# The down projection of a decoder layer: other sums around its seven products, the weight sums made by DMAs in DRAM

## The chip, the cores and the metric

The kernel runs on one core of one Trainium2 chip. The metric is the device time of one execution in microseconds (us), median over several. The core has five engines that run their own instruction queues in order: TensorE (PE, with its weight loads PEld), VectorE (DVE), ScalarE (ACT), GpSimd (POOL) and SyncE (SP). SP, ACT and POOL also issue DMAs.

## The reference, cut to what matters

One decoder layer: a token mixer, a cross-attention and a gated MLP. The change touches the last matrix product, `(silu(a) * b) @ w_down`, that is 1024 x 2816 times 2816 x 1024.

```python
def conv_glu_ffn(h, w_up, conv_w, conv_b, w_down):
    u = causal_dwconv(h @ w_up, conv_w) + conv_b
    a, b = jnp.split(u, 2, axis=-1)
    return (jax.nn.silu(a) * b) @ w_down
...
    y = conv_glu_ffn(rmsnorm(h, g[4]), ffn_w_up[l], ffn_conv_w[l], ffn_conv_b[l], ffn_w_down[l])
    h = h + rmsnorm(y, g[5])
```

The input projection, `z = h @ w_in` at the layer's start, is where the change puts new DMAs.

## The kernel before

All data is float32. A product of two float32 matrices is made of three matmuls (`mm3`, lines 238 to 241): each operand is split into a high part in float32r, which ACT copies out, and a low part, which DVE makes by a subtraction, and the products high-high, high-low and low-high are added in PSUM. So each 128 x 512 operand tile costs ACT one copy and DVE one subtraction before TensorE can use it.

The stages that matter here run in this order.

**Input projection** (loop at line 670, 22 steps in `in_order`). Each step multiplies one 128-column slice of `w_in` with the whole normed input. `weight` (line 154) loads the weights two steps ahead and splits them into a tile of tag `w`, of which there are four (line 145), so a tile is used again four steps later. DVE also computes the depthwise convolution taps (line 355) and, behind step 13, a small triangular inverse, `base_inverse` (line 656), in a tile `b_ca` that POOL sets to zero and one first (lines 651, 652). From its end the scan of the next stage follows.

**Up projection** (lines 1243 to 1275). It writes the 22 tiles of the gated activations to DRAM (`mid_d`), which are 128 channels x 1024 tokens each.

**Down projection** (from line 1282). A is `mid_d`, B is `w_down`; both are cut in 2 x 2 blocks, for each of the 11 pairs of channel tiles `kp`. Seven block products (`PRODS`, a Strassen scheme) stand for the eight of the plain rule: 7 products x 11 steps x 4 row blocks x 3 = 924 matmuls of 512 columns. `down_operands` (line 1317) prepares one step: it loads one or two blocks of `w_down` by SP, adds them on DVE where there are two (line 1328), subtracts two blocks of A where there are two (line 1335), and splits the pair into a tile of tag `w` (lines 133 and 134 for a pair of sums, 1339 and 1340 otherwise). `a_block` loads each A block once, by SP. `fetch` keeps up to four steps prepared, and three steps of the last product in extra tiles (`EXTRA`). At the last step of a product `done` (line 1373) moves the four PSUM banks into the accumulators `yacc`, by ACT copies or DVE additions (line 1349). A list `pend` holds the normalisation work, which is put between the steps. The last six steps of the last product run one row block after the other, so that each block's end (line 1355) can begin while the next is multiplied.

The program is written in this order, and a planner places each engine's instructions, so neighbouring steps interleave. An engine that waits holds up all that is behind it in its queue.

Of the kernel before, what the change touches and what calls it, by code (L numbers as in the profile page):

```python
# [7 lines left out]
F32 = mybir.dt.float32  # L8
F32R = mybir.dt.float32r
I32 = mybir.dt.int32  # L10
AF = mybir.ActivationFunctionType
# [5 lines left out]
P = 128  # L17
T = 1024
D = 1024
# [50 lines left out]
def hybrid_layer(  # L70
# [69 lines left out]
    def raw_tile(shape, name):  # L140
        return wpool.tile(list(shape), F32, tag="raw", name=f"raw_{name}", bufs=2)
# [403 lines left out]
    def flush(keep=0):  # L545
        while len(pend) > keep:
            pend.pop(0)()
# [108 lines left out]
    def base_inverse():  # L656
# [9 lines left out]
            dve.tensor_tensor(bx[:, 0:k, k:B], bx[:, 0:k, k:B], t_, op=ALU.add)  # L666
        sync.dma_start(out=blocks(x_d), in_=bx)

    kinds = {"q": query, "k": key, "v": value, "g": gate, "a": glu_conv, "b": glu_gate}
# [597 lines left out]
    for j in range(PLAIN, NFF):  # L1267
# [6 lines left out]
        if j == PLAIN:  # L1274
# [4 lines left out]

    dr = ctx.enter_context(pool("dr", side="right"))
    dl = ctx.enter_context(pool("dl"))
    g5 = row_gain(5, gbp)
# [2 lines left out]
    ss5 = small(NC * 2, "ss5", bufs=1)  # L1287
    LAST = 6


    PRODS = (("M4", 0, ("22",), ("21", "11")), ("M3", 1, ("11",), ("12", "22")),
             ("M2", 0, ("22", "21"), ("11",)), ("M1", 1, ("11", "22"), ("11", "22")),
             ("M6", 0, ("21", "11"), ("11", "12")), ("M5", 0, ("11", "12"), ("22",)),
             ("M7", 1, ("12", "22"), ("21", "22")))
    ENDP = len(PRODS) - 1

    EXTRA = (5, 6, 7)
    res = {}

    def a_block(b, kp):  # L1300

        if (b, kp) not in res:
            if b == "21":
                if kp % 4 == 0:
                    g = dl.tile([P, 4, 512], F32, tag="a21", name=f"ma21_{kp}", bufs=3)
                    for i in range(4):
                        res[b, "t", kp + i] = g[:, i]
                t = res[b, "t", kp]
            else:
                t = (dr if b == "22" and kp < 8 else dl).tile([P, 512], F32, name=f"ma{b}_{kp}")  # L1310
            res[b, kp] = t
            sync.dma_start(out=t, in_=mid_d[2 * kp + int(b[1]) - 1][:, HS[int(b[0]) - 1]])
        return res[b, kp]

    n_step = [0]

    def down_operands(m, kp):
        name, _, ab, bb = PRODS[m]
        p, tag, bufs = (wpool, "raw", 2) if n_step[0] % 3 == 0 else (dr, "braw", 4)
        n_step[0] += 1  # L1320
        A_s = [a_block(b, kp) for b in ab]
        rb = p.tile([P, 2, 512], F32, tag=tag, name=f"rb{name}_{kp}", bufs=bufs)

        at = lambda b: w_down[2 * kp + int(b[0]) - 1][:, HS[int(b[1]) - 1]]
        sync.dma_start(out=rb[:, 1], in_=at(bb[0]))
        if len(bb) == 2:
            sync.dma_start(out=rb[:, 0], in_=at(bb[1]))
            dve.tensor_tensor(rb[:, 1], rb[:, 1], rb[:, 0], op=ALU.subtract if name == "M1" else ALU.add)
# [5 lines left out]
        if len(ab) == 2:  # L1334
            dve.tensor_tensor(rb[:, 0], A_s[0], A_s[1], op=ALU.subtract)
            split(w, rb)
        else:
            for i, r in enumerate((A_s[0], rb[:, 1])):
                act.activation(w[:, 0, i], r, AF.Copy)
                dve.tensor_tensor(w[:, 1, i], r, w[:, 0, i], op=ALU.subtract)  # L1340
        return w

    def square(t, n):
        jk = dl.tile([P, 512], F32, tag="junk", name="sqj", bufs=2)
        act.activation(jk, yacc[t][:, HS[n]], AF.Square, accum_out=ss5[:, 2 * t + n:2 * t + n + 1])

    def add_to(t, n, o, sign=1):
        y = yacc[t][:, HS[n]]
        dve.tensor_tensor(y, y, o, op=ALU.add if sign > 0 else ALU.subtract)

    def gained(t, n):
        y = yacc[t][:, HS[n]]
        dve.tensor_tensor(y, y, g5[:, HS[n]], op=ALU.mult)

    def final(t, fin, first):

# [9 lines left out]
        return s1  # L1366

    def residual(t, last=False):
        fin = raw_tile((P, D), f"fin{t}") if last else dl.tile([P, D], F32, tag="fin", name=f"fin{t}", bufs=2)
        sync.dma_start(out=fin, in_=h2_d[t])  # L1370
        return fin

    def done(name, q, o):

        lo, hi = q, q + 4
        if name == "M4":
            act.activation(yacc[hi][:, HS[0]], o, AF.Copy)
            act.activation(yacc[lo][:, HS[0]], o, AF.Copy)
        elif name == "M3":
            act.activation(yacc[lo][:, HS[1]], o, AF.Copy)  # L1380
            act.activation(yacc[hi][:, HS[1]], o, AF.Copy)
        elif name == "M2":
            add_to(hi, 0, o, -1)
            square(hi, 0)
            pend.append(lambda: gained(hi, 0))
        elif name == "M1":
            add_to(hi, 1, o)
        elif name == "M6":
            add_to(hi, 1, o)
            square(hi, 1)  # L1390
            pend.append(lambda: (gained(hi, 1), final(hi, residual(hi), 0)))
        elif name == "M5":
            add_to(lo, 0, o)
            add_to(lo, 1, o, -1)
            square(lo, 1)
            pend.append(lambda: gained(lo, 1))
        else:
            add_to(lo, 0, o)
            square(lo, 0)
            gained(lo, 0)  # L1400
            final(lo, fins.pop(lo), 1)

    fins = {}
    todo = [(m, kp) for m in range(ENDP) for kp in range(NP)]
# [13 lines left out]
        mm3(o, w[:, 0, 0, s], w[:, 1, 0, s], w[:, 0, 1], w[:, 1, 1], start, stop, onto)  # L1418

    banks = [None, None]  # L1420
    for m, (name, bset, _, _) in enumerate(PRODS):
        onto = name in ("M6", "M7")
        if not onto:
            banks[bset] = [psum("b", f"{name}_{q}") for q in range(4)]
        o = banks[bset]
# [9 lines left out]
                pend.pop(0)()  # L1435
    flush()
    fetch()
    fins.update({q: residual(q, q > 1) for q in range(4)})
    for q in range(4):
        for kp in range(NP - LAST, NP):  # L1440
            step_mm(banks[1][q], dops[ENDP, kp], q, False, kp == NP - 1, True)
        done("M7", q, banks[1][q])
    psum_es[0].close()


# [60 lines left out]
```

## Time and profile before

| | us |
|---|---|
| median of 3 runs | 1478.18 |
| the 3 runs | 1476.74, 1478.18, 1485.74 |
| the profiled execution, its own time | 1477.1 |
| its span, first to last instruction | 1475.1 |
| TensorE busy in the span | 1428.7 (97%) |
| VectorE busy | 1162.9 (79%) |
| ScalarE busy | 694.7 (47%) |
| GpSimd busy | 150.5 (10%) |

The span is the time from the first to the last instruction; 2.0 us of the execution lie around it. Matmuls are pipelined: one is shown as 0.39 us long, but the next begins some 0.227 us later. "Clock" is the granted TensorE clock, 1.00 is 2.4 GHz and 0.5 is 1.2 GHz.

### The profile page before, as it was taken

How to read it: one execution, taken by the hardware profiler on the slowest of the kernel's cores; microseconds unless marked ns; L12 is line 12 of the kernel's file. 1: busy time of each engine (PE TensorE's matmuls, PEld its weight loads, DVE VectorE, ACT ScalarE, POOL GpSimd, SP SyncE). 2: the span in 40 equal slices, each digit the busy share in tenths (PEclk: the TensorE clock that was granted, in tenths of full speed). 3: DMA queues.
4: the chain of work that ended last, by engine and by line, in shares of the span. 5: the costliest groups of instructions: out<-in, count | busy, mean ns of one | idle time of the engine just before them, and what ended most of it. 6: DMA issues, size and time to landing. Idle time of an engine off the chain costs nothing.

```text
span 1475.1 us, 19398 instructions
## 1 busy us (share of the span) xinstructions
PE 1428.7 (97%) x7087; PEld 1183.2 (80%) x7087; DVE 1162.9 (79%) x1971; ACT 694.7 (47%) x1309; POOL 150.5 (10%) x102
## 2 busy tenths in 40 slices
PE   6999999999999999999999999999999998999996
PEld 6878888888898878878788788888888886888875
DVE  6699999993567778743567988888888887879997
ACT  6526463642566545432534554444444444554442
POOL 0000000000000000000001233333333330000000
PEclk9999999999999999999999999999999999999998
DMA  7533233328756766410424522222222226985473
GB/s 251 165 96 94 79 101 80 120 99 266 245 169 204 244 223 189 127 68 1 157 101 143 171 100 72 86 86 79 79 72 86 86 84 202 343 291 187 144 251 112
DMA packets 121631, 212.01 MB, mean 144 GB/s; under 512 B 17440, under 2 KB 61120, under 8 KB 121536
## 3 DMA queue, kind: packets, MB, share of 16 engines
q1 hardware_dynamic: 97600, 159.13, 34.7%
q10 hardware_dynamic: 22976, 48.51, 8.8%
q0 software_dynamic: 960, 3.15, 0.7%
q8 instruction: 55, 0.90, 0.3%
q14 instruction: 40, 0.33, 0.1%
HBM read 156.73 MB, written 54.02 MB: 143 GB/s over the span
## 4 chain that ended last, share of the span: by engine, by line
PE 80%; DVE 7%; DMA 7%; ACT 2%; issue 2%; SPq 0%; DVEq 0%; ACTq 0%
PE st L239 9%; PE st L241 9%; PE st L240 8%; PE pj L241 6%; PE pj L239 6%; PE pj L240 6%; PE M L240 4%; PE M L241 3%; PE M L239 3%; PE y L240 2%; PE y L241 2%; PE y L239 2%; PE sc L240 1%; PE sc L241 1%; PE sc L239 1%
## 5 line engine op out<-in xcount | busy, mean ns | idle before, releaser
L241 PE MATMUL pj<-xT,w_in 128*128 128x512 f32 x384 | 150.3, 391 | 1.1 <-DVE w_in L134 1.1
L239 PE MATMUL pj<-xT,w_in 128*128 128x512 f32 x384 | 150.8, 393 | 0.1
L355 DVE SCALAR_TENSOR_TENSOR ca<-sg,par,ca 128x1023 f32<-128x1023 f32 (+18 forms) x120 | 149.9, 1264 | 1.1
L240 PE MATMUL pj<-xT,w_in 128*128 128x512 f32 x384 | 149.9, 390 | 0.0
L240 PE MATMUL M<-wM 128*128 128x512 f32 x308 | 121.3, 394 | 4.2 <-DVE wM L1340 2.7
L239 PE MATMUL st<-xT,wst 128*128 128x512 f32 x320 | 125.0, 391 | 0.0
L241 PE MATMUL st<-xT,wst 128*128 128x512 f32 x320 | 124.7, 390 | 0.0
L240 PE MATMUL st<-xT,wst 128*128 128x512 f32 x320 | 124.4, 389 | 0.0
L239 PE MATMUL M<-wM 128*128 128x512 f32 x308 | 119.5, 394 | 4.4 <-ACT wM L133 3.4
L241 PE MATMUL M<-wM 128*128 128x512 f32 x308 | 121.0, 393 | 0.0
L1156 DVE SCALAR_TENSOR_TENSOR ua<-ua,par 128x1023 f32<-128x1023 f32 x88 | 112.5, 1281 | 10.3 <-ACT ua L1154 7.4
L239 PE MATMUL st<-x,wst 128*128 128x512 f32 x240 | 96.8, 403 | 0.0
L241 PE MATMUL st<-x,wst 128*128 128x512 f32 x240 | 94.7, 394 | 0.0
L240 PE MATMUL st<-x,wst 128*128 128x512 f32 x240 | 94.2, 393 | 0.0
L133 ACT ACTIVATE wM<-rbM 128x1024 fp32r<-128x1024 f32 x55 | 57.9, 1062 | 74.8 <-PE M L241 51.8
L1186 DVE TENSOR_TENSOR wst<-sums,wst 128x512 fp32r<-128x512 f32 x80 | 63.5, 816 | 34.4 <-ACT wst L1185 34.3
L1185 ACT ACTIVATE wst<-sums 128x512 fp32r<-128x512 f32 x80 | 46.0, 620 | 91.1 <-POOL sums L1180 91.1
L241 PEld LDWEIGHTS pj<-xT,w_in 128*128 128x128 f32 x384 | 72.1, 188 | 15.9 <-DVE w_in L134 1.3
L239 PEld LDWEIGHTS pj<-xT,w_in 128*128 128x128 f32 x384 | 72.1, 188 | 14.9 <-ACT w_in L133 0.3
L240 PEld LDWEIGHTS pj<-xT,w_in 128*128 128x128 f32 x384 | 72.2, 188 | 14.5
L134 DVE TENSOR_TENSOR wM<-rbM,wM 128x1024 fp32r<-128x1024 f32 x55 | 66.7, 1221 | 8.7 <-ACT wM L133 8.7
L240 PEld LDWEIGHTS M<-wM 128*128 128x128 f32 x308 | 58.4, 190 | 18.2 <-DVE wM L1340 3.6
(383 smaller groups left out, 3566.0 us busy)
## 6 DMA issues: line engine op xcount, KB each, us to landing
rbM<-in_w_down SPq DMA_DIRECT2D x132, 256.0 KB, 3.9
raw_up<-in_w_up SPq DMA_DIRECT2D x44, 512.0 KB, 3.6
raw_in<-in_w_in SPq DMA_DIRECT2D x24, 512.0 KB, 3.7
mid_d<-ua ACTq DMA_DIRECT2D x22, 512.0 KB, 2.6
ma<-mid_d SPq DMA_DIRECT2D x44, 256.0 KB, 5.4
raw_kv<-in_w_kv SPq DMA_DIRECT2D x16, 512.0 KB, 4.0
h_d<-h ACTq DMA_DIRECT2D x16, 512.0 KB, 2.7
xr<-in_x ACTq DMA_DIRECT2D x8, 512.0 KB, 4.8
```

The lines of the kernel that those rows point to most:

```text
L133: act.activation(w[:, 0], raw, AF.Copy)
L134: dve.tensor_tensor(w[:, 1], raw, w[:, 0], op=ALU.subtract)
L239: pe.matmul(o, lhsT=wh, rhs=xh, start=start, stop=False, skip_group_check=onto)
L240: pe.matmul(o, lhsT=wh, rhs=xl, start=False, stop=False, skip_group_check=onto)
L241: pe.matmul(o, lhsT=wl, rhs=xh, start=False, stop=stop, skip_group_check=onto)
L355: dve.scalar_tensor_tensor(out=ca[:, d:], in0=sg[:, :T - d], scalar=par[:, wb + 30 - d:wb + 31 - d], in1=ca[:, d:], op0=ALU.mult, op1=ALU.add)
L1156: dve.scalar_tensor_tensor(out=a[:, d:], in0=u[:, :T - d], scalar=fw(2 - d), in1=a[:, d:], op0=ALU.mult, op1=ALU.add)
L1185: act.activation(w[:, i, 0], op[s], AF.Copy)
L1186: dve.tensor_tensor(w[:, i, 1], op[s], w[:, i, 0], op=ALU.subtract)
```

## The change

Another scheme with seven products: `P1` and `P2` add into the same PSUM banks, as do `P4` and `P5`, and `P6` and `P7`, each right after the other. On the A side the sums are made in place in the loaded blocks (two DVE operations in each step of `P2`, two in each of `P3`), and used again. On the B side four products take a sum of blocks (`T1` to `T4`). These 44 sums are made in DRAM, in 22 steps of the input projection: POOL reads a word of the step's weight tile (`mark`), and behind that issues four DMAs of 256 KB, plain copies and DMAs that add onto what is there (`accum_op`). The second to fourth of them read or add to what an earlier one has written. In the down projection SP loads one B tile in each step; POOL issues the loads of the A blocks "21" and "22". The row normalisation's multiply becomes a scalar_tensor_tensor with a sign.

```diff
+    td_d = [[dram.tile([P, 512], F32, name=f"td_d{k}_{i}") for i in range(4)] for k in range(NFF // 2)]
...
+    def weight_sums(n, name):
+        kp, part = divmod(n, 2)
+        if kp >= NFF // 2:
+            return
+        t1, t3, t2, t4 = td_d[kp]
+        dma = nc.gpsimd.dma_start
+        mark = small(1, "mark")
+        ins = nc.gpsimd.tensor_copy(mark, w_ready[name][:, 0, 0:1].bitcast(F32))
+        with tc.issue_after(ins.ins):
+            if part == 0:
+                dma(out=t1, in_=w_block(kp, "11"))
+                dma(out=t3, in_=w_block(kp, "12"))
+                dma(out=t1, in_=w_block(kp, "12"), accum_op=ALU.add)
+                dma(out=t3, in_=w_block(kp, "22"), accum_op=ALU.add)
+            else:
+                dma(out=t2, in_=t1)
+                dma(out=t2, in_=w_block(kp, "22"), accum_op=ALU.add)
+                dma(out=t4, in_=t2)
+                dma(out=t4, in_=w_block(kp, "21"), accum_op=ALU.add)
...
     for n, (kind, i) in enumerate(in_order):
         before = len(pend)
         kinds[kind](i)
+        weight_sums(n, f"in{col[kind] + i}")
...
+    PRODS = (("P1", 0, False, "11", "B11"), ("P2", 0, True, "12", "B21"), ("P3", 1, False, "S2", "T2"),
+             ("P4", 0, False, "21", "T1"), ("P5", 0, True, "12", "B22"), ("P6", 1, False, "11", "T3"),
+             ("P7", 1, True, "22", "T4"))
...
+    for kp in (0, 2):
+        g = raw_tile((P, 2, 512), f"ma11_{kp}")
...
+            (nc.gpsimd if b in ("21", "22") else sync).dma_start(
+                out=ma[b, kp], in_=mid_d[2 * kp + int(b[1]) - 1][:, HS[int(b[0]) - 1]])
...
+        rb = dr.tile([P, 512], F32, tag="braw", name=f"rb{name}_{kp}", bufs=6)
+        sync.dma_start(out=rb, in_=w_block(kp, b[1:]) if b[0] == "B" else
+                       td_d[kp][("T1", "T3", "T2", "T4").index(b)])
+        if name in ("P1", "P2"):
+            a_block({"P1": "21", "P2": "22"}[name], kp)
...
+        if name == "P3":
+            tt_(A, a_block("22", kp), a_block("11", kp), op=ALU.add)
+        for i, r in enumerate((A, rb)):
+            act.activation(w[:, 0, i], r, AF.Copy)
+            tt_(w[:, 1, i], r, w[:, 0, i], op=ALU.subtract)
+        if name == "P2":
+            tt_(a_block("11", kp), a_block("11", kp), a_block("21", kp), op=ALU.subtract)
+            tt_(a_block("21", kp), a_block("22", kp), a_block("21", kp), op=ALU.subtract)
+        elif name == "P3":
+            tt_(a_block("12", kp), A, a_block("12", kp), op=ALU.subtract)
...
+        if name == "P1":
             act.activation(yacc[hi][:, HS[0]], o, AF.Copy)
+        elif name == "P2":
             act.activation(yacc[lo][:, HS[0]], o, AF.Copy)
+            square(lo, 0)
+            pend.append(lambda: gained(lo, 0))
+        elif name == "P3":
+            add_to(hi, 0, o, alu=ALU.subtract)
+        elif name == "P4":
+            add_to(hi, 0, o, 1)
+        elif name == "P5":
+            dve.tensor_tensor(yacc[lo][:, HS[1]], yacc[hi][:, HS[0]], o, op=ALU.add)
...
-    for m, (name, bset, _, _) in enumerate(PRODS):
-        onto = name in ("M6", "M7")
+    for m, (name, bset, onto, _, _) in enumerate(PRODS):
```

## Rows read from the trace of the kernel before

**Rows 1.** Stretches of the down stage: busy us, PEclk, DMA share, GB/s
```profile
1250.00:1260.00 10.00, 7.46 (x32) 5.82 (x32) 10.00 (x16) 3.98 (x7) 0.00 (x0) 1.00 0.80 257
1260.00:1270.00 10.00, 10.00 (x46) 8.29 (x45) 8.59 (x14) 4.48 (x8) 0.00 (x0) 1.00 1.04 385
...
1420.00:1440.00 20.00, 16.25 (x69) 12.29 (x67) 19.99 (x34) 8.30 (x14) 0.00 (x0) 1.00 0.83 279
1440.00:1450.00 10.00, 8.83 (x28) 6.91 (x28) 10.00 (x14) 4.01 (x4) 0.00 (x0) 0.67 0.32 99
```

**Rows 2.** What TensorE waited for from 1236 us: total, times, longest
```profile
PE M L239 <- ACT wM L133: 3.4, 1, 3.4
PE M L240 <- DVE wM L1340: 2.7, 2, 1.7
PE M L240 <- DVE wM L134: 1.5, 1, 1.5
PE M L239 <- ACT wM L1339: 0.9, 1, 0.9
```

**Rows 3.** Timeline of TensorE, down stage: start, us, instruction, idle before and releaser
```profile
1242.71 0.50 PE L239 MATMUL M<-wM 128*128 128x512 f32 x1
...
1441.17 1.65 PE L239 MATMUL M<-wM 128*128 128x512 f32 x3 [3.43 <-ACT wM L133]
...
1463.82 0.39 PE L240 MATMUL M<-wM 128*128 128x512 f32 x1
...
1465.41 0.39 PE L241 MATMUL M<-wM 128*128 128x512 f32 x1
```

**Rows 4.** Groups by line, 1180 to 1475 us: busy, mean ns, idle before
```profile
L134 DVE TENSOR_TENSOR wM<-rbM,wM 128x1024 fp32r<-128x1024 f32 x55 | 66.7, 1221 | 8.7 <-ACT wM L133 8.7
...
L1328 DVE TENSOR_TENSOR rbM<-rbM 128x512 f32<-128x512 f32 x55 | 37.5, 687 | 9.7 <-DMA rbM<-in_w_down 9.3
L1335 DVE TENSOR_TENSOR rbM<-ma,ma 128x512 f32<-128x512 f32 x55 | 36.9, 687 | 0.3
...
L1340 DVE TENSOR_TENSOR wM<-ma,wM 128x512 fp32r<-128x512 f32 x22 | 15.2, 689 | 6.9 <-ACT wM L1339 6.0 <-DMA rbM<-in_w_down 0.7
```

**Rows 5.** Timeline of VectorE at the end of product M5
```profile
1433.89 4.27 DVE L1349 TENSOR_TENSOR yacc<-yacc,M 128x512 f32<-128x512 f32 x7
```

**Rows 6.** DMA issues by line: queue, count, KB each, median us to landing
```profile
ma<-mid_d SPq DMA_DIRECT2D x44, 256.0 KB, 5.4
...
xt_d<-xt POOLq DMA_DIRECT2D x12, 256.0 KB, 3.4
xT<-xt_d SPq DMA_DIRECT2D x4, 768.0 KB, 9.6
...
u_d<-U SPq DMA_DIRECT2D x8, 256.0 KB, 2.4
```

**Rows 7.** Timeline of GpSimd: its work from 200 to 790 us
```profile
258.97 0.95 POOL L651 MEMSET b_ca<- 128x1024 f32 x1 [239.17 <-DMA cv_d<-ca]
...
787.67 2.32 POOL L1113 DMA_DIRECT2D xt_d<-xt  x3 [527.54 <-DVE pn_y L218]
```

**Rows 8.** Timeline of ScalarE: weight tiles split, of 25 between 63 and 345 us
```profile
63.80 1.05 ACT L133 ACTIVATE w_in<-raw_in 128x1024 fp32r<-128x1024 f32 x1
...
249.75 1.05 ACT L133 ACTIVATE w_in<-raw_in 128x1024 fp32r<-128x1024 f32 x1
...
309.35 1.12 ACT L133 ACTIVATE w_in<-raw_in 128x1024 fp32r<-128x1024 f32 x1
...
340.75 1.05 ACT L133 ACTIVATE kvw<-raw_kvr 128x1024 fp32r<-128x1024 f32 x1
```

**Rows 9.** Timeline of VectorE: the first read of the tile that GpSimd sets
```profile
285.12 0.19 DVE L660 COPY b_ca<-b_sg 128x31 f32<-128x31 f32 x1
```

**Rows 10.** Stretches of the input projection and behind it: columns as in Rows 1
```profile
300.00:320.00 20.00, 20.00 (x98) 16.74 (x97) 20.00 (x29) 8.93 (x22) 0.00 (x0) 1.00 0.28 98
...
360.00:380.00 20.00, 17.30 (x147) 16.11 (x145) 9.86 (x12) 11.17 (x18) 0.00 (x0) 0.91 1.06 351
```

More of the change, by code (lines that the diff above doesn't have):

```diff
@@ L667, in base_inverse, with w_block @@
         sync.dma_start(out=blocks(x_d), in_=bx)
+    def w_block(kp, b):
+        return w_down[2 * kp + int(b[0]) - 1][:, HS[int(b[1]) - 1]]
+    def weight_sums(n, name):
[17 more added lines that the diff above has]
+                dma(out=t4, in_=w_block(kp, "21"), accum_op=ALU.add)
     kinds = {"q": query, "k": key, "v": value, "g": gate, "a": glu_conv, "b": glu_gate}
@@ L1288, in hybrid_layer @@
     LAST = 6
[L1291 to L1294, printed above, removed]
+    ma = {}
+    for b, kps in (("12", range(NP)), ("22", range(8, NP))):
+        for kp in kps:
+            ma[b, kp] = dl.tile([P, 512], F32, name=f"ma{b}_{kp}")
+    junk = [dl.tile([P, 512], F32, name=f"sqj{i}") for i in range(2)]
@@ new lines, in hybrid_layer @@
+    finp = [dl.tile([P, D], F32, name=f"fin{i}") for i in range(2)]
+    for kp in range(4, NP):
+        ma["11", kp] = dl.tile([P, 512], F32, name=f"ma11_{kp}")
+    for kp in range(8):
+        ma["22", kp] = dr.tile([P, 512], F32, name=f"ma22_{kp}")
+    for kp in range(0, NP, 4):
+        g = dl.tile([P, 4, 512], F32, tag="a21", name=f"ma21_{kp}", bufs=3)
+        for i in range(4):
+            ma["21", kp + i] = g[:, i]
+    for kp in (0, 2):
+        g = raw_tile((P, 2, 512), f"ma11_{kp}")
+        for i in range(2):
+            ma["11", kp + i] = g[:, i]
@@ L1295, in hybrid_layer @@
+    PRODS = (("P1", 0, False, "11", "B11"), ("P2", 0, True, "12", "B21"), ("P3", 1, False, "S2", "T2"),
+             ("P4", 0, False, "21", "T1"), ("P5", 0, True, "12", "B22"), ("P6", 1, False, "11", "T3"),
+             ("P7", 1, True, "22", "T4"))
     ENDP = len(PRODS) - 1
     EXTRA = (5, 6, 7)
-    res = {}
+    loaded = set()
     def a_block(b, kp):
[L1302 to L1313, printed above, removed]
@@ L1315, in hybrid_layer @@
-    n_step = [0]
-    def down_operands(m, kp):
[L1318 to L1328, printed above, removed]
+        if (b, kp) not in loaded:
+            loaded.add((b, kp))
+            (nc.gpsimd if b in ("21", "22") else sync).dma_start(
+                out=ma[b, kp], in_=mid_d[2 * kp + int(b[1]) - 1][:, HS[int(b[0]) - 1]])
@@ new lines, in a_block @@
+        return ma[b, kp]
+    def down_operands(m, kp):
+        name, _, _, a, b = PRODS[m]
+        A = a_block(a, kp) if a != "S2" else dr.tile([P, 512], F32, tag="s2", name=f"s2_{kp}", bufs=2)
+        rb = dr.tile([P, 512], F32, tag="braw", name=f"rb{name}_{kp}", bufs=6)
[3 more added lines that the diff above has]
+            a_block({"P1": "21", "P2": "22"}[name], kp)
@@ L1332, in down_operands, with add_to @@
             w = wpool.tile([P, 2, 2, 512], F32R, tag="w", name=f"w{name}_{kp}", bufs=4)
[L1334 to L1340, printed above, removed]
+        tt_ = dve.tensor_tensor
+        if name == "P3":
[8 more added lines that the diff above has]
+            tt_(a_block("12", kp), A, a_block("12", kp), op=ALU.subtract)
         return w
     def square(t, n):
[L1344 to L1349, printed above, removed]
+        act.activation(junk[n], yacc[t][:, HS[n]], AF.Square, accum_out=ss5[:, 2 * t + n:2 * t + n + 1])
+    def add_to(t, n, o, to=None, alu=ALU.add):
+        y = yacc[t]
+        dve.tensor_tensor(y[:, HS[n if to is None else to]], y[:, HS[n]], o, op=alu)
     def gained(t, n):
         y = yacc[t][:, HS[n]]
-        dve.tensor_tensor(y, y, g5[:, HS[n]], op=ALU.mult)
+        dve.scalar_tensor_tensor(out=y, in0=y, scalar=(1.0, -1.0)[n], in1=g5[:, HS[n]], op0=ALU.mult, op1=ALU.mult)
     def final(t, fin, first):
@@ L1368, in residual @@
     def residual(t, last=False):
-        fin = raw_tile((P, D), f"fin{t}") if last else dl.tile([P, D], F32, tag="fin", name=f"fin{t}", bufs=2)
+        fin = raw_tile((P, D), f"fin{t}") if last else finp[t % 2]
         sync.dma_start(out=fin, in_=h2_d[t])
@@ L1437, in hybrid_layer @@
     fetch()
-    fins.update({q: residual(q, q > 1) for q in range(4)})
+    fins.update({q: residual(q, q > 5) for q in range(4, 8)})
     for q in range(4):
@@ L1441, in hybrid_layer @@
             step_mm(banks[1][q], dops[ENDP, kp], q, False, kp == NP - 1, True)
-        done("M7", q, banks[1][q])
+        done("P7", q, banks[1][q])
     psum_es[0].close()
```

29 lines of the change are left out of this document (8 added, 21 removed).

## The prediction

> **What bounds the kernel now.** I read the page first: TensorE is busy 97% of the span, so a change can only give back idle TensorE time or take matmuls away. It takes none away: seven products of 11 steps stand before and after, 924 matmuls. Next I read the stretches of the down stage. The reader is to see that TensorE has no idle time in the middle, and loses some at the entry (7.46 of 10 us busy) and at the end (16.25 of 20, then 8.83 of 10 at a granted clock of 0.67, so partly at the 1.2 GHz level) [rows 1]. DVE is full in these same stretches: 10.00 of 10 and 19.99 of 20.
>
> Then the whole stage. Its first matmul starts at 1242.71 and its last at 1465.41, 222.7 us [rows 3]. Undisturbed starts lie 0.227 us apart (1463.82 to 1465.41 are seven), and 923 x 0.227 = 209.5. So 13.2 us are lost, and that is all the down stage can give. The list of waits names 8.5 of them: 3.4, 2.7, 1.5 and 0.9, always for a split operand, made by ACT or DVE [rows 2]. The other 4.7 I put down to the low clock behind the longest wait and to slow starts after waits. The longest, 3.43 us, ends at 1441.17 [rows 3]; just before it DVE ran seven additions of product M5 in a row from 1433.89, 4.27 us [rows 5], with the operands of the last product queued behind them. The rest of the time, from 1465.8 to the end, is the last block's normalisation and store, which the change keeps.
>
> **The change: DVE and ACT in the down stage.** Before, DVE prepares the steps with 55 subtractions of a pair (1221 ns), 55 + 55 sums (687) and 44 single subtractions (about 688): 66.7 + 37.5 + 36.9 + 30.3 = 171.4 us [rows 4]. After: two subtractions in each of 77 steps, two sums more in each of the 22 steps of P2 and P3, so 198 operations of 687 ns = 136.0 us. DVE is relieved of 35.4 us. Additions into the accumulators go from 24 to 20, and the worst end of a product has four, not eight. ACT gets 154 copies of half a pair for 55 of a pair and 44 of half a pair, which lies beside the matmuls, as ACT is busy under half the time. The sign in the normalisation's multiply costs nothing worth naming; it is an instruction of the same size.
>
> Where does this count? TensorE needs 12 x 0.227 = 2.72 us for a step. DVE needs four operations in P2 and P3, at most 4 x 0.687 = 2.75 by their durations, which overlap a little in its queue; these are the tight products, and up to three steps are prepared ahead. From P4 on it is 1.4 us a step. So at the end, where DVE was full, it now has half its time free, and the 3.4 and 1.5 us waits and the low clock behind them should go. At the entry DVE still does the last convolutions of the up stage, but the sums of B are gone from there, and the first four A blocks go to the buffers of the up weights, which are free early. Of the entry's waits (2.7 + 0.9, bounds 0 and 3.6) I leave 1.2.
>
> **What it adds in the down stage.** Three times a product now adds onto the banks of the one just finished, so the first matmul of each row block waits until ACT (P1 to P2) or DVE (P4 to P5, P6 to P7) has read its bank. The three other row blocks, 9 x 0.227 = 2.0 us, lie between. DVE needs one addition, 0.69, and up to two operand operations ahead of it in the queue, 1.4: about 2.1. So each boundary costs between 0 and one such operation per row block, 4 x 0.69 = 2.8; since it all but fits, I take 1.0 for the three. Behind a held matmul wait all of TensorE's later ones.
>
> The A blocks "21" and "22" are loaded by POOL: 22 issues of about 0.77 us (2.32 for three [rows 7]) are 17 us, ahead of the 60 us of P1 and P2. A load lands in 3.4 to 5.4 us [rows 6]. If one were late, DVE would wait in P2 with all splits behind it; I take 0. The bytes of the first two products stay at three blocks a step, the DMA engines are full there now (share 1.04) and TensorE does not stop for it [rows 1]. SP's issues for operands fall from 176 to 99.
>
> **What it adds in the input projection.** 22 marks and 88 DMAs of 256 KB on POOL. POOL has nothing to do there but two memsets, and its own sums and stores come after 787 us [rows 7], so its time is free; the T sums are read some 900 us later. The DMA share is 0.28 there [rows 10]; each weight load has its buffer two steps ahead. But a dependent DMA must wait for the landing of the one before, in POOL's queue, and two things queue behind it. First the marks: each reads a weight tile, which is overwritten four splits later, so a late mark holds up ACT's split, and TensorE behind it. Second the memset of `b_ca`, which DVE reads at 285.12 [rows 9].
>
> A pair of steps has five landings in series (t1 copied and added to, t2 copied and added to, t4 copied) and two issues that nothing hides, 1.5 us. A plain copy from DRAM to DRAM is not in this trace; a 256 KB store by POOL lands in 3.4 us, bounds 2.4 and 5.4 [rows 6]. An adding DMA isn't in it either. Below it is 3.4, as a plain one. Above it is 9.6: the landing of a transfer of 768 KB [rows 6], as much as two reads and a write move together. I take 5.0, nearer to the plain one, since that has the same queue, size and target. With a for the addition, a pair costs 3 x 3.4 + 2a + 1.5 = 11.7 + 2a, so 21.7 us. The marks come every (309.35 - 63.80) / 21 = 11.7 us [rows 8], a pair every 23.4. So the chain keeps up, and it costs nothing but some contention; I put 0.4 for that.
>
> The Trainium skill, "Collectives: The Full Stack", on the bandwidth ceiling, says that an adding transfer is about half as fast as a copy because it reads two sources, not because adding takes time. With the formula of "DMA: Bandwidth & Descriptors" (Anatomy of one DMA), 2.0 us plus bytes / 436 GB/s, an estimate by these pages is 2.6 us for a copy and 3.2 for an addition, a pair of 15.7 us, and the chain would be hidden still more safely. The second page also says (Two DMAs through the same engine are not ordered) that the issuer has to wait on the first DMA's semaphore; that is the rule against this change, and no row here shows its price.
>
> **Sum.** 1477.1 - 13.2 + 1.2 (entry) + 1.0 (boundaries) + 0.4 = 1466.5 us, on the profiled execution, which lies 1.1 below the median of 1478.18; against that median it is 0.8% less.
>
> **Rivals.**
> 1. *The additions are slow and POOL's chain paces the input projection (slower).* 18 weight tiles are split before the memset's 258.97 (the 18th at 249.75 [rows 7, 8]), so up to 18 marks and their DMAs, nine pairs, stand ahead of it from 65 us on. It is late by 65 + 9 x (11.7 + 2a) - 285 = 18a - 115, so from a = 6.4 us on, and each us more costs 18. The weight tiles bind later: mark 20 must run by the split at 340.75 [rows 8], 65 + 10 x (11.7 + 2a) = 341, a = 8.0. At a = 8.0 the DVE queue is held 29 us, which gives 1495; at 9.6, 58 us, 1524. For it: the price is unknown, and DVE is 20.00 of 20 busy there [rows 10], so a delay isn't made good. Against: the store by POOL of 3.4. Between 6.4 and 7.9 the time stays under 1493.
> 2. *The chained boundaries take the gain back.* With 2.8 us each, 8.4, the entry's 3.6 unchanged, 1477.1 - 13.2 + 8.4 + 3.6 + 0.4 = 1476.3. For it: DVE's queue is in order; against: the 2.0 us between, and DVE half free from P4 on.
> 3. *All 13.2 come back, and the last normalisations run a little more freely.* 1462 to 1463.5. For it: the last block's addition had to wait for DVE's work on the block before.
>
> **Chances.** Forecast 0.50, rival 1 0.30 (0.12 of it under 1493), rival 2 0.12, rival 3 0.08. About 1% is what a measurement here can tell from no change: 1463.4 and 1493.0 around the median. Faster by over 1%: rival 3 and a little of the forecast, 0.15. Slower by over 1%: the rest of rival 1, 0.18. Within: 0.67. The forecast's own range is 1463.5 to 1472. The wide one goes from 1461 to 1494, past rivals 2 and 3 and into rival 1, leaving out some 0.18, mostly its slow end.
>
> **What would show it.** Right: no wait of TensorE over 1 us from 1420 on, clock 1.00 in the last 40 us, first to last matmul of the stage near 211.5 us, the input projection ending when it did, POOL's memset before 285. Wrong: a mark that ACT's split waits for, the first `b_ca` read much after 285, an adding DMA of over 6.4 us, waits of TensorE for `yacc` where a product adds onto its predecessor, or work of DVE in P2 and P3 that falls behind.

## The result and the profile after: 0.7% slower

The median of the changed kernel is 1490.63 us, beside 1480.73 us for the kernel before on the same chips; the ratio is 1.0066, with an interval of 1.0046 to 1.0086. So it is slower by some 10 us, where 0.8% faster was forecast. The two profiled executions lie further apart than the medians, 1477.1 and 1493.74 us by their own times (spans 1475.1 and 1492.0), so the stages below add up to 16.9, not to 10, and single microseconds of them aren't to be trusted.

| point in the program | before | after | later by |
|---|---|---|---|
| SP issues the store of the inverse (`x_d` from `b_ca`), end of the input projection | 336.51 | 351.90 | 15.4 |
| first store of `xt_d` by POOL [rows 7] | 787.67 | 805.80 | 18.1 |
| first matmul of the down stage [rows 3] | 1242.71 | 1260.86 | 18.2 |
| last matmul [rows 3] | 1465.41 | 1481.55 | 16.1 |
| end of the span | 1475.1 | 1492.0 | 16.9 |

Most of the loss, 15.4 us, is there by the end of the input projection. The down stage gives 2.0 us back (222.7 to 220.7), where 11.0 were forecast. Stretches after; the columns are those of [rows 1] (busy us of TensorE, its weight loads, DVE, ACT and POOL, then the clock, the DMA share and GB/s):

```profile
70.00:80.00 10.00, 10.00 (x55) 8.65 (x55) 9.82 (x12) 1.75 (x3) 4.63 (x8) 1.00 0.84 209
80.00:90.00 10.00, 10.00 (x45) 5.25 (x44) 1.15 (x1) 0.00 (x0) 3.02 (x4) 1.00 1.05 294
90.00:100.00 10.00, 5.83 (x21) 3.91 (x19) 8.11 (x7) 5.04 (x7) 1.44 (x3) 0.72 0.82 198
300.00:320.00 20.00, 20.00 (x108) 17.18 (x109) 19.48 (x34) 9.09 (x31) 3.72 (x6) 1.00 0.64 177
360.00:380.00 20.00, 18.64 (x137) 17.47 (x135) 5.57 (x6) 6.02 (x9) 0.00 (x0) 1.00 0.95 313
1260.00:1270.00 10.00, 8.54 (x35) 5.93 (x34) 8.22 (x10) 7.21 (x10) 4.83 (x9) 1.00 1.03 401
1270.00:1280.00 10.00, 4.83 (x20) 3.41 (x19) 3.73 (x6) 1.02 (x2) 0.54 (x1) 0.94 1.04 400
1280.00:1290.00 10.00, 10.00 (x33) 7.94 (x33) 9.30 (x16) 5.05 (x10) 0.00 (x0) 0.72 0.92 318
1420.00:1440.00 20.00, 20.00 (x90) 16.55 (x89) 19.64 (x47) 14.37 (x31) 0.00 (x0) 1.00 0.70 230
1460.00:1480.00 20.00, 20.00 (x90) 16.55 (x89) 10.22 (x23) 4.62 (x11) 0.00 (x0) 1.00 0.11 40
```

The end of the down stage is as clean as forecast: TensorE full and at 1.00 where it had 16.25 of 20 and a clock of 0.67 [rows 1]. The entry is worse than before: 1.5 and 5.2 us idle, and behind that 33 matmuls in ten microseconds at a clock of 0.72, where 46 fit. The input projection has a hole at 80 to 100 us: DVE does 1.15 of 10 and TensorE then 5.83 of 10. The same stretch of the kernel before, in which DVE never stops:

```profile
70.00:80.00 10.00, 10.00 (x57) 8.76 (x56) 9.86 (x11) 3.21 (x4) 0.00 (x0) 1.00 1.04 325
80.00:90.00 10.00, 10.00 (x45) 5.48 (x44) 9.86 (x9) 2.13 (x3) 0.00 (x0) 1.00 0.29 80
```

The timeline after tells how both holes come about (start, length, engine, instruction, and the idle time before it with its releaser; SPq is SP's queue):

```profile
64.40 1.24 POOL L683 COPY mark<-w_in 128x1 f32<-128x1 f32 x1 [63.28 <-ACT w_in L134]
...
70.63 0.87 POOL L688 DMA_DIRECT2D td_d<-in_w_down  x1 [3.85 <-DMA td_d<-in_w_down]
...
71.77 1.55 POOL L584 MEMSET zero<- 128x1024 f32 x1
...
73.34 6.85 SPq L586 DMA_DIRECT2D x_d<-zero  x4
80.29 3.13 SPq L162 DMA_DIRECT2D raw_in<-in_w_in  x1
...
90.69 1.06 ACT L134 ACTIVATE w_in<-raw_in 128x1024 fp32r<-128x1024 f32 x1 [12.19 <-DMA raw_in<-in_w_in]
...
91.78 1.23 DVE L135 TENSOR_TENSOR w_in<-raw_in,w_in 128x1024 fp32r<-128x1024 f32 x1 [10.63 <-ACT w_in L134]
...
283.43 0.98 POOL L652 MEMSET b_ca<- 128x1024 f32 x1
...
300.52 0.20 DVE L661 COPY b_ca<-b_sg 128x31 f32<-128x31 f32 x1 [1.20 <-DMA b_sg<-u_d]
...
1255.33 18.15 SPq L1359 DMA_DIRECT2D rbP<-in_w_down  x11
...
1271.60 0.33 ACTq L1191 DMA_DIRECT2D mid_d<-ua  x1
...
1273.54 5.16 SPq L1351 DMA_DIRECT2D ma<-mid_d  x8
...
1278.98 0.63 ACT L1372 ACTIVATE wP<-ma 128x512 fp32r<-128x512 f32 x1 [10.79 <-DMA ma<-mid_d]
...
1279.66 0.80 PE L240 MATMUL P<-wP 128*128 128x512 f32 x1 [4.88 <-ACT wP L1372]
```

In the input projection the planner put the memset of the tile `zero` behind the first mark and its four DMAs: 71.77, where it had run at 18.84. SP's four stores of zeros wait for it (73.34, before 66.56), and the weight load behind them in SP's queue goes out at 80.29, before at 72.12. It also lands late. ACT waits 12.19 us for it and DVE 10.63 for ACT. DVE is full up to 340 us, so it can't make that up. The memset of `b_ca`, which the prediction watched, is in time, but not by much. It is 17 us ahead of its reader, which is itself 15.4 us later than before; it runs 24.5 us later than before, and only 1.7 us ahead of the reader's old time [rows 7, 9].

In the down stage the fifth A block, `ma11_4`, the first one that isn't in the early buffers, is issued at 1273.54. It stands on SP behind eleven loads of weight blocks; the first six of these go out from 1255.33 on, and the others wait until a split frees one of the six buffers. Meanwhile POOL's 22 loads fill the DMA engines (share 1.03 and 1.04). `ma11_4` did not wait for the store of the up stage's last result: ACT issues that store at 1271.60, and it takes 5.8 us to land, so it was still under way when `ma11_4` went out.

What the DMAs cost others, by the list of DMA issues (queue, count, KB each, median us to landing), for [rows 6]:

```profile
td_d<-in_w_down POOLq DMA_DIRECT2D x66, 256.0 KB, 5.1
raw_in<-in_w_in SPq DMA_DIRECT2D x20, 512.0 KB, 4.4
td_d<-td_d POOLq DMA_DIRECT2D x22, 256.0 KB, 3.2
x_d<-zero SPq DMA_DIRECT2D x4, 512.0 KB, 9.1
dec<-gc_d SPq DMA_DIRECT2D x4, 512.0 KB, 8.7
...
u_d<-U SPq DMA_DIRECT2D x8, 256.0 KB, 4.6
```

The adding DMAs are about as fast as assumed: 5.1 us for 44 of them and 22 plain copies in one row. By their lines, the four groups of eleven additions have medians of 4.8 to 6.0 us, and the copies in that row 4.8 and 5.1. The 22 copies from `td_d` land in 3.2. But `u_d` now lands in 4.6, before 2.4 [rows 6], the zeros in 9.1, before 5.9, and `dec` in 8.7, before 5.9.

### The profile page after: what moved, and what is told of

Read it like the earlier page. It is cut to its first block, busy times and chain, and to the rows that moved or that the text cites. A ratio compares the mean times of both kernels' runs of the same rounds, so it can differ in the third digit from the quotient of the medians.

```text
span 1492.0 us, 19519 instructions
## 1 busy us (share of the span) xinstructions
PE 1436.7 (96%) x7087; PEld 1189.9 (80%) x7087; DVE 1126.4 (76%) x1956; ACT 695.6 (47%) x1356; POOL 239.5 (16%) x234
## 4 chain that ended last, share of the span: by engine, by line
PE 58%; DVE 2%; DMA 1%; ACT 1%; issue 1%; SPq 0%; DVEq 0%; ACTq 0%
PE st L240 9%; PE st L241 8%; PE st L242 8%; PE P L240 4%; PE P L241 4%; PE P L242 4%; PE y L241 2%; PE y L240 2%; PE y L242 2%; PE sc L240 2%; PE sc L241 2%; PE sc L242 2%; PE wo L242 1%; PE wo L241 1%; PE wo L240 1%; PE up L240 1%
## 5 line engine op out<-in xcount | busy, mean ns | idle before, releaser
L242 PE MATMUL pj<-xT,w_in 128*128 128x512 f32 x384 | 152.1, 396 | 1.1 <-DVE w_in L135 1.1
L240 PE MATMUL pj<-xT,w_in 128*128 128x512 f32 x384 | 153.0, 399 | 0.1
L241 PE MATMUL pj<-xT,w_in 128*128 128x512 f32 x384 | 151.9, 396 | 0.0
L240 PE MATMUL P<-wP 128*128 128x512 f32 x308 | 121.0, 394 | 5.1 <-ACT wP L1372 4.9
L241 PE MATMUL P<-wP 128*128 128x512 f32 x308 | 121.4, 394 | 1.7 <-DVE wP L1373 1.7
L1184 DVE SCALAR_TENSOR_TENSOR ua<-ua,par 128x1023 f32<-128x1023 f32 x88 | 112.6, 1280 | 11.4 <-ACT ua L1182 8.3
L242 PE MATMUL P<-wP 128*128 128x512 f32 x308 | 120.9, 392 | 0.0
L1141 POOL DMA_DIRECT2D xt_d<-xt x12 | 8.8, 763 | 490.6 <-DVE pn_y L219 474.1
L242 PEld LDWEIGHTS pj<-xT,w_in 128*128 128x128 f32 x384 | 73.4, 191 | 16.3 <-DVE w_in L135 1.3
L240 PEld LDWEIGHTS pj<-xT,w_in 128*128 128x128 f32 x384 | 73.4, 191 | 15.4 <-ACT w_in L134 0.3
L241 PEld LDWEIGHTS pj<-xT,w_in 128*128 128x128 f32 x384 | 73.3, 191 | 14.9 <-issue 0.3
L1208 POOL TENSOR_TENSOR sums<-raw_up 128x512 f32<-128x512 f32 x20 | 37.4, 1868 | 254.9 <-DMA raw_up<-in_w_up 245.0
L240 PEld LDWEIGHTS P<-wP 128*128 128x128 f32 x308 | 58.5, 190 | 18.8 <-ACT wP L1372 5.8
```

The source lines that it names most:

```text
L240: pe.matmul(o, lhsT=wh, rhs=xh, start=start, stop=False, skip_group_check=onto)
L241: pe.matmul(o, lhsT=wh, rhs=xl, start=False, stop=False, skip_group_check=onto)
L242: pe.matmul(o, lhsT=wl, rhs=xh, start=False, stop=stop, skip_group_check=onto)
L1141: nc.gpsimd.dma_start(out=xt_d[i][:, :, s], in_=v[i])
L1184: dve.scalar_tensor_tensor(out=a[:, d:], in0=u[:, :T - d], scalar=fw(2 - d), in1=a[:, d:], op0=ALU.mult, op1=ALU.add)
L1208: nc.gpsimd.tensor_tensor(op[s], op[p], op[m], op=alu)
```

## The experiments

Two questions: what do the sums cost, and by what (the order of the queues or the traffic); and where did the down stage's gain go. In `e1_no_sums`, `e6_entry`, `e8_small_sums`, `e9_late_loads` and `e10_small_zero_first` the products that should use the sums take a plain block.

| kernel | median us | ratio to before | interval |
|---|---|---|---|
| changed kernel | 1490.63 | 1.0066 | 1.0046 to 1.0086 |
| e1_no_sums | 1478.58 | 0.9985 | 0.9973 to 0.9998 |
| e2_sums_only | 1494.45 | 1.0093 | 1.0072 to 1.0113 |
| e3_zero_first | 1487.75 | 1.0052 | 1.0035 to 1.0069 |
| e4_later | 1490.59 | 1.0072 | 1.0055 to 1.0089 |
| e5_up_stage | 1491.06 | 1.0074 | 1.0046 to 1.0102 |
| e6_entry | 1473.41 | 0.9964 | 0.9947 to 0.9982 |
| e7_both | 1485.5 | 1.0032 | 1.0013 to 1.0051 |
| e8_small_sums | 1484.24 | 1.0024 | 1.0003 to 1.0045 |
| e9_late_loads | 1466.75 | 0.9906 | 0.9891 to 0.992 |
| e10_small_zero_first | 1477.86 | 0.9981 | 0.9967 to 0.9995 |
| e11_sbuf_sums | 1499.18 | 1.0136 | 1.0113 to 1.0159 |
| e12_two_gaps | 1475.41 | 0.9961 | 0.9948 to 0.9975 |

Differences of ratios below are turned into microseconds with 1480.7; 0.001 is 1.5 us. Intervals of that size or twice that stand behind each ratio, so two rows tell apart some 3 to 5 us.

**One half alone.**

```diff
-        weight_sums(n, f"in{col[kind] + i}")
...
-        sync.dma_start(out=rb, in_=w_block(kp, b[1:]) if b[0] == "B" else td_d[kp][...])
+        sync.dma_start(out=rb, in_=w_block(kp, b[1:] if b[0] == "B" else "11"))
```

> The changed kernel without the marks and the 88 DMAs that make the sums; the four products that take a sum load a plain block of w_down of the same size, so the output is another one. Theory: the whole loss (15.4 us by the end of the triangular inverse) comes from these DMAs in the input projection, and the new down projection alone gains about 2 us. Then this takes 15 to 18 us less than the changed kernel, some 1474 to 1478, and the store of the inverse is issued near 336 us as before. Rival: the marks and DMAs cost nothing and the loss comes from another placement of instructions; then this is within 4 us of the changed kernel.

And the kernel before with the marks and DMAs of the diff, whose results nobody reads:

> The kernel before, with the marks and the 88 DMAs added and their results not read. Theory: 14 to 18 us slower than before (about 1494 to 1498), with the store of the inverse near 352 us. Rival (the loss needs the new down projection): within 4 us of before.

The sums cost 1.0066 - 0.9985 = 0.0081, 12 us, in the changed kernel, and 0.0093, 14 us, in the kernel before. The new down projection alone is worth 2 us. The plain block in the place of the sums makes no difference of its own: the down stage takes 220.9 us in `e1_no_sums` and 220.7 in the changed kernel.

**The order on POOL.** The memset of `zero` ahead of the first mark:

```diff
+    zero_set = nc.gpsimd.memset(zero, 0.0)
...
+        with tc.issue_after(zero_set.ins):
             ins = nc.gpsimd.tensor_copy(mark, ...)
```

> The changed kernel with POOL's memset of the zero tile put ahead of its first mark; all DMAs stay. Theory A (order): the memset stood behind the first mark and four DMAs, so the four zero stores held SP's queue until 73.3 us and the weight loads behind them; with it first the zero stores go out at 66.6 us and 6 to 15 us come back, 1476 to 1485. Theory B (traffic): the zero stores and weight loads are late because the sums' DMAs share the engines with them between 65 and 100 us; then at most 5 us come back, 1486 to 1490, and ScalarE still waits some 10 us for a weight load near 80 to 90 us.

The zeros' stores went out at 66.57 again, and yet only 0.0014, 2 us, came back, less than two rows tell apart; the inverse was stored at 348.17. So the order alone isn't it. Then the same DMAs with an eighth of the bytes, in all eight lines alike:

```diff
-                dma(out=t1, in_=w_block(kp, "11"))
+                dma(out=t1[0:16], in_=w_block(kp, "11")[0:16])
...
```

> The changed kernel with the same 88 DMAs at the same places and with the same marks, each over 16 of 128 partitions (an eighth of the bytes); the products that should use the sums take a plain block of the weight, so the output differs. Theory (bytes): 10 of the 12 us come back, 1478 to 1481 us, and raw_in lands as fast as before (at most 7.0 us). Rival (order: the marks on POOL and what waits behind them, the memset of the zero tile and the stores on SP): 1485 to 1490, as with the full sums, with SP's stores of the zeros at 72 us or later and ACT's wait of 10 us or more for raw_in.

It came out between the two expectations, and the fourth corner of the square, both edits together, settles it:

> The changed kernel with the 88 DMAs over 16 of 128 partitions and, besides, the memset of the zero tile ahead of the first mark on POOL; the products that should use the sums take a plain block of the weight, so the output differs. With the runs so far it makes the four of a square: full or small DMAs, memset behind or ahead of the first mark (0.0066, 0.0024 and 0.0052 over before; without any sums 0.0015 under it). Theory (two separate costs, some 6 us of bytes and some 6 us of order, the latter from the zeros' stores on SP at 73.8 us): 1477 to 1480 us (0.997 to 1.000), the stores of the zeros at 66 to 67 us, raw_in at 72 to 73, and the store of the inverse at 336 to 338. Rival (what is left at small bytes comes from the DMAs of POOL themselves, not from the memset): 1482 to 1485, the inverse at 340 or later.

The timeline of SP in `e10_small_zero_first`:

```profile
66.53 5.64 SPq L586 DMA_DIRECT2D x_d<-zero  x4
72.26 10.86 SPq L162 DMA_DIRECT2D raw_in<-in_w_in  x3
...
336.39 0.38 SPq L668 DMA_DIRECT2D x_d<-b_ca  x1
```

All three as before the change, and the time is that of no sums (0.9981 and 0.9985). So 88 marks and issues on POOL cost nothing by themselves. The bytes cost 0.0042 where the memset is late and 0.0071 where it isn't, 6 to 11 us; the late memset costs 0.0014 where the bytes are full and 0.0043 where they are few, 2 to 6 us. The two overlap, since both delay the same weight load. ACT waited for `raw_in` as follows (total, times, longest) in the changed kernel, with the memset early, and with few bytes; with both it did not wait for it at all, as before.

```profile
ACT w_in L134 <- DMA raw_in<-in_w_in: 13.2, 2, 12.2
ACT w_in L134 <- DMA raw_in<-in_w_in: 10.9, 3, 9.4
ACT w_in L134 <- DMA raw_in<-in_w_in: 5.8, 1, 5.8
```

The longest of these waits ends at 90.69, 88.39 and 85.35 us, each time ahead of the same split. Whether 88 plain copies of the same size would cost as much as copies and additions, no run tells.

**Other places for the traffic.** If the bytes cost because they meet a stretch that is full already (66 to 100 us here), a later start should help:

```diff
-        weight_sums(n, f"in{col[kind] + i}")
+        for m in ([n - 5] if 5 <= n < 17 else [2 * n - 22, 2 * n - 21] if n >= 17 else []):
+            weight_sums(m, f"in{col[kind] + i}")
```

> The changed kernel with the sums begun five steps later (the last ten parts two to a step), so that no sum's DMA runs before some 85 to 100 us. Theory B: the crowded stretch from 65 to 100 us is as before, the early loss of some 10 us is gone: 1476 to 1482, unless the doubled parts at the end delay the stage behind 340 us. Theory A: the same, since POOL's memset is no longer behind anything. This one tells whether the loss is tied to the first 100 us (it is by both) or grows with every DMA (then 1487 to 1491).

The input projection was untouched (inverse at 336.63). But the DMAs now ran on past 340 us, and there the stretches show

```profile
340.00:360.00 20.00, 19.54 (x119) 17.22 (x117) 4.97 (x5) 5.49 (x8) 3.53 (x8) 1.00 1.03 277
360.00:380.00 20.00, 10.42 (x64) 9.89 (x65) 6.12 (x8) 5.25 (x8) 2.54 (x5) 0.76 1.06 357
```

with TensorE at 10.42, before 17.30 [rows 10]. The same loss in another place. So I moved the sums to the up projection, where the DMA share is 0.25 for 360 us, each DMA one step behind the one that it depends on:

```diff
             ins = nc.gpsimd.tensor_tensor(op[s], op[p], op[m], op=alu)
+        weight_sums(j - PLAIN, ins)
```

> The 88 sum DMAs are issued in the up projection (840 to 1220 us), behind POOL's four sums of each step, each DMA one step (20 us) behind the one it depends on; nothing else differs from the changed kernel. Theory (the 12 us are collisions of the sums' bytes with the loads of 66 to 100 us and of 340 to 400 us): the DMA share of the up projection is 0.24 to 0.28 there, the sums take it to about 0.7, and PE stays full; the time comes down to that of the kernel without sums, 1477 to 1480 us (0.997 to 1.000 of before), with the store of the inverse on SP at 336 to 337 us. Rival (the sums cost their time wherever they lie, since loads under a running stream of DRAM-to-DRAM traffic land later): 1484 to 1492, with PE waits for wst in the up projection.

The rival holds: 0.0089 over no sums, 13 us. The list of DMA issues of 880 to 1080 us, and what TensorE and POOL waited for there; the last row is the load in `e1_no_sums`, without the sums:

```profile
td_d<-in_w_down POOLq DMA_DIRECT2D x54, 256.0 KB, 5.6
raw_up<-in_w_up SPq DMA_DIRECT2D x19, 512.0 KB, 6.8
...
PE st L240 <- DVE u L1235: 7.1, 7, 1.7
POOL sums L1209 <- DMA raw_up<-in_w_up: 67.7, 7, 10.6
...
raw_up<-in_w_up SPq DMA_DIRECT2D x20, 512.0 KB, 3.6
```

The share there is 0.63 to 0.65, far from full, but `raw_up` lands in 6.8 us for 3.6 without the sums. POOL's own queue isn't the limit: in seven of the ten steps POOL sits idle until these loads land. Each of these loads is issued when its buffer comes free and is wanted at once: POOL's sums, ACT's and DVE's splits and TensorE stand in line behind it. So TensorE waits about 1 us in each of seven steps, and does 192.2 us of work from 900 to 1100, where it does 200.0 without the sums. A DMA share says how much could still be moved, not whether a load can afford to land later. The Trainium skill, "DMA: Bandwidth & Descriptors" (Queues, rings and completion order), says that each DMA engine takes turns between the queues that have work for it, packet by packet. The trace agrees as far as it goes: the sums are in another queue than SP's loads, and the loads get slower by 3.2 us under them instead of going first. It does not show the turns themselves.

**The entry of the down stage.** Some A blocks change places between the pools `dl` and `dr`, on the kernel without sums:

```diff
-    for kp in range(4, NP):
-        ma["11", kp] = dl.tile(...)
-    for kp in range(8):
-        ma["22", kp] = dr.tile(...)
+    for b, kps in (("11", range(4, NP)), ("22", (NP - 1,))):
+        for kp in kps:
+            ma[b, kp] = dr.tile(...)
```

> The kernel without sums (the products that should use them take a plain block of the weight, so the output differs), and in it the A blocks ma11_4 to ma11_10 change places with ma22_0 to ma22_7: they lie where the tiles of the input of the up projection end earlier, not where its last result lies. Theory (the entry of the down projection lost about 11 us of PE because ma11_4 waited on SP for the last store of the up projection, behind eleven weight loads): the loads of ma11_4 and on are issued between the weight loads from 1240 us, PE has no 4 to 5 us wait at its fifth step and the clock stays at 1.00; 5 to 9 us less than without the swap, 1469 to 1474 us (0.992 to 0.995 of before). Rival (the DMA share of 1.0 in the entry is the limit in any order, since POOL's 22 loads of 256 KB run there too): within 2 us of the kernel without sums, 1477 to 1480.

SP now issues `ma11_4` at 1240.28, between the weight blocks, and the stage takes 213.4 us for 220.9. But its first matmul comes 3.1 us later than in `e1_no_sums`, since ACT waits for the first weight block, which is loaded beside POOL's loads:

```profile
1245.76 0.63 ACT L1368 ACTIVATE wP<-rbP 128x512 fp32r<-128x512 f32 x1 [6.89 <-DMA rbP<-in_w_down]
...
PE P L239 <- ACT wP L1368: 2.7, 1, 2.7
```

By the ratios 0.0021, 3 us, came back, about as much as two rows tell apart. The expectation gave a wrong reason for the old order, the wait for the last store; what the trace shows of the swap is that `ma11_4` got an earlier place in SP's queue. So POOL's 22 loads were each put behind a copy that reads the split of their step:

```diff
-        if name in ("P1", "P2"):
-            a_block({"P1": "21", "P2": "22"}[name], kp)
...
+        if name in ("P1", "P2"):
+            with tc.issue_after(marks[-1]) if marks else ExitStack():
+                ins = nc.gpsimd.tensor_copy(mark, w[:, 0, 1, 0:1].bitcast(F32))
+            with tc.issue_after(ins.ins):
+                marks.append(nc.gpsimd.dma_start(out=ma[b, kp], in_=...).ins)
```

> The kernel without sums and with the A blocks swapped (so the output differs as there), and in it POOL's 22 loads of ma21 and ma22 are each issued behind a small copy on POOL that reads the split weight block of their step in P1 and P2, so they no longer run ahead of the first weight blocks. Theory (in the swapped kernel the first weight block of the down projection was issued at 1238.3 us and split at 1245.8, since POOL's loads, from 1233 us on, fill the DMA engines, share 1.03): ACT splits the first weight block 3 to 5 us sooner, PE's wait of 2.7 us at the entry goes and the clock stays 1.00; 1468 to 1472 us (0.991 to 0.994 of before). Rival (ma21 then comes late for DVE's differences, or the entry is held by ACT and DVE alone): 1473 to 1476 (0.995 to 0.997).

This is the largest gain of any edit that takes no work away: 0.0058 more, 9 us, and 12 us for both edits. The first to the last matmul of the stage is 1243.91 to 1454.87, 211.0 us. The wait of ACT for the first weight block, and all that TensorE waited for from 1236 us to the end:

```profile
1241.63 0.63 ACT L1366 ACTIVATE wP<-rbP 128x512 fp32r<-128x512 f32 x1 [2.38 <-DMA rbP<-in_w_down]
...
PE P L240 <- DVE wP L1367: 0.2, 1, 0.2
```

With the swap alone on the kernel that sums in the up projection:

> The changed kernel with both: the sums in the up projection, and the A blocks swapped. If both theories hold: 1469 to 1474 us, 0.992 to 0.995 of before and 16 to 21 us less than the changed kernel. If the sums cost their time anywhere: 1480 to 1486. If only the entry's theory falls: 1477 to 1480.

It took 0.0042 off that kernel, and the sums still cost 0.0032 + 0.0036 = 0.0068 there, 10 us.

**Whole versions.** First without any DMA from DRAM to DRAM: adding DMAs into the tile in which the block lands, in the down stage itself, where POOL is idle and the DMA share is 0.41 (1300 to 1440 us); the sum of P3 is stored to DRAM once, for P7:

```diff
+    PARTS = {"P3": ("11", "12", "22"), "P4": ("11", "12"), "P6": ("12", "22"), "P7": ("t2", "21")}
...
+                marks.append(nc.gpsimd.dma_start(out=r, in_=source(s[1], b), accum_op=ALU.add).ins)
```

> A whole version: no sums in DRAM during the input projection; the sums of the weights are made as the blocks are loaded in the down projection, by adding DMAs from DRAM into the tile that SP's load has filled (two of them a step in P3, one a step in P4, P6 and P7; P3's sum goes back to DRAM once for P7), issued by POOL one step behind the load; A blocks swapped and POOL's loads of them late. Theory (the DMA share in the down projection is 0.4, POOL is idle there, and the step of 2.7 us leaves room for an adding DMA of about 5 us that is issued two to four steps ahead): as the kernel without sums and with both repairs, plus 0 to 2 us: 1468 to 1474 (0.991 to 0.996). Rival (POOL's chain waits for each landing in turn, and two adding DMAs take longer than a step): PE waits for wP in P3 of more than 1 us a step, 1480 to 1500.

```profile
1300.00:1330.00 30.00, 21.99 (x85) 16.33 (x84) 19.62 (x31) 11.84 (x25) 11.59 (x14) 0.94 1.07 248
...
q0 software_dynamic: 2118, 3.98, 74.3%
q1 hardware_dynamic: 992, 1.81, 17.8%
...
rbP<-in_w_down POOLq DMA_DIRECT2D x55, 256.0 KB, 6.2
```

The rival again: in P3, with two additions a step, TensorE does 22 of 30 us, and the DMA engines are full at 248 GB/s, where plain loads moved 401 in as full a stretch of the changed kernel. The queue rows of the same 30 us (packets, MB, share of the 16 engines) say why. POOL's queue q0, in which all DMAs of this stretch but one are additions, takes 74.3% for 3.98 MB, SP's loads in q1 17.8% for 1.81 MB: 5.6 and 3.0 us of the engines per MB. In the changed kernel, from 1260 to 1270 us, both queues carry plain loads, and these rows give 2.5 and 2.6:

```profile
q0 software_dynamic: 826, 2.72, 69.2%
q1 hardware_dynamic: 695, 1.26, 33.3%
```

So it isn't POOL's queue: by the profile's count of bytes, an added byte holds the engines some 1.9 times as long as a loaded one, near the half speed that the prediction quotes. Not all of the loss need be that, since SP also waited 21.0 of the 30 us for stores of sums, whose buffers its next loads use.

Last, the sums split over two stretches (T1, T3 and the copy of T1 by the first line, the rest by the second), and both repairs of the entry:

```diff
+        if n >= 5:
+            weight_sums(n - 5, w_ready[f"in{col[kind] + i}"][:, 0, 0:1].bitcast(F32))
...
+        weight_sums_2(t, nb[:, 0:1])
```

> The changed kernel whole, with both repairs of the entry (A blocks swapped, POOL's 22 loads of them behind the split weight blocks), and with the 88 sum DMAs in two stretches: T1, T3 and the copy of T1 (55 of them) from the sixth step of the input projection on, about 100 to 250 us, each DMA one step behind the one it depends on; the other 33 behind the eight score products at 640 to 700 us, where the trace of before has a DMA share of 0.00. Theory (what the sums cost depends on which loads they meet: none that is due within its own landing time at 100 to 340 us, none at all at 640 to 700): the store of the inverse on SP at 336 to 338 us, xt_d at 787 to 791, no wait of PE over 1 us from 1240 us on; 1466 to 1471 us, 0.990 to 0.993 of before, as the kernel without sums and with both repairs. Rival (the sums cost 12 us in any place, as they did in the input projection and in the up projection): 1477 to 1481.

0.9961: faster than before by 6 us and than the changed kernel by 16, and so the best whole version here. But neither number was met: the sums still cost 0.9961 - 0.9906 = 0.0055, 8 us, more than the 0 to 4 of the theory; that it is less than the 12 of the first place, these intervals don't show. Its profile shows 5.4 of them: `xt_d` is stored 3.4 us later than in `e9_late_loads`, and the down stage takes 212.8 us for 211.0, with one wait that `e9_late_loads` doesn't have, for DVE's addition of `P6` (`add_to`), where `P7` adds onto its bank. Just before, DVE had stood 4 us for a residual (`fin`, line 1418), with the operand work and then the addition behind it in its queue:

```profile
1424.57 1.41 DVE L1418 SCALAR_TENSOR_TENSOR fin<-yacc,r_y,fin 128x512 f32<-128x512 f32 x2 [4.01 <-DMA fin<-h_d]
...
1430.41 0.47 PE L240 MATMUL P<-wP 128*128 128x512 f32 x1 [2.23 <-DVE yacc L1407]
```

The other 2 to 3 us are no more than the 2.7 by which this profiled execution (1472.71) lies under its median. Where exactly the 3.4 arise stays open.

## Why the prediction was wrong, step by step

- **The end of the down stage: right.** With DVE relieved, no wait of over 1 us is left from 1300 us on and the clock stays at 1.00, as the prediction said one would see.
- **The chained banks, 1.0 us: right in size.** The changed kernel shows no wait there. `e3_zero_first`, `e12_two_gaps` and `e11_sbuf_sums` show one each, of 1.8, 2.2 and 7.1 us, always where `P7` adds onto `P6`. So the mechanism of rival 2 exists, at one boundary of three, and its size hangs on what stands ahead of the addition in DVE's queue.
- **The entry, 1.2 us: mis-sized.** The stage lost 220.7 - 209.5 = 11.2, nearly all of it before 1290. The prediction reasoned that the sums of B are gone and that the first four A blocks have early buffers. It never asked for the fifth, and what stands ahead of it on SP: eleven weight loads, and a wait of TensorE of 4.88 us. And it took POOL's 22 loads as hidden ("ahead of the 60 us of P1 and P2", "TensorE does not stop for it") because the DMA engines were as full before; but before, all these loads stood in SP's one queue, and none came from a second queue beside the ones that were wanted first. `e9_late_loads` takes both away and ends at 211.0 us, where the prediction's terms gave 209.5 + 1.2 + 1.0 = 211.7.
- **The contention in the input projection, 0.4 us: the step that turned the sign.** It measured 12 us as a whole. The prediction read the DMA share from one stretch, 300 to 320 us, "0.28 there" [rows 10]. At 70 to 80 us the share was 1.04 already, just where the first marks start. And the better question, which loads are wanted as soon as they land, wasn't asked; it is what the up projection answers, with a share of 0.25 and the same cost.
- **What queues on POOL: right idea, wrong memset.** The prediction followed the memset of `b_ca`. It didn't look at that of `zero`, which had run at 18.84, long before the first mark, and which the planner moved behind it. By the square of four kernels that is 2 to 6 of the 12.
- **The price of an adding DMA, 5.0 us: right** (5.1 in a row of 44 additions and 22 copies, 4.8 to 6.0 by lines). So rival 1 fell: the chain kept pace, its last DMA was issued at 337.67, and the memset of `b_ca` was in time. It fell narrowly: by the prediction's sum the memset comes at 65 + 9 x 21.7 = 260, and it came at 283.43, partly because its marks waited for splits that were late themselves. That the time lies in the part of the range that was held open for rival 1 is luck; it got there for another reason. The formula of the Trainium skill ("DMA: Bandwidth & Descriptors", Anatomy of one DMA), by which the estimates were 2.6 and 3.2 us, is short of both rows, 3.2 for a copy and 5.1 for the mixed row; these ran beside other traffic.
- **The sum.** 1466.5 was forecast, and `e9_late_loads`, the new down projection with its entry mended and no sums at all, takes 1466.75. The closeness of these two is partly luck, since the sum starts from a profiled execution that lies some 4 us under the median of its kernel (1477.1, and 1481.47 in the round of `e9_late_loads`). From profile to profile the gain is 10.2 us for a forecast of 10.6, by the ratio 14. Still, the prediction priced a kernel in which nothing collides. What was wrong in it were the prices of the two collisions, some 12 us for each.

## What to carry to other kernels

A low DMA share doesn't make background DMAs free: before placing them, look for the loads that are waited for as soon as they land, and count how much later each may be. When loads are given to another queue "early", ask which more urgent load they now share the engines with; tying each to the step that makes it due was worth 9 us here. And when a helper puts work into an engine's queue, follow everything that the planner may move behind it, also what ran long before.

## What the runs showed of the hardware that I had not expected

- Loads on SP land later under POOL's traffic even when the DMA engines have room: `raw_up` of 512 KB 6.8 us for 3.6, at a share of 0.65.
- Adding DMAs into SBUF, beside plain loads and stores, filled the DMA engines (share 1.07) at 248 GB/s; plain loads reached 401 GB/s at 1.03. By the profile's count of bytes an added one held the engines some 1.9 times as long as a loaded one (5.6 and 3.0 us per MB).
- DMAs of POOL of 32 KB instead of 256 KB, 88 of them with 22 marks, cost nothing measurable (0.9981 for 0.9985), once the memset of `zero` stood ahead of them.
- The granted clock was lower behind the longer holes of TensorE, so partly at the 1.2 GHz level: 0.72 from 1280 to 1290 us, behind 5.2 us of idle time, and 0.76 and 0.73 in the two stretches from 360 to 400 us of `e4_later`, where TensorE did 10.42 of the first 20 us. The 33 matmuls at 0.72, where 46 fit, cost about 3 us (13 x 0.227).
